# Softmax times values on one core: values of four heads loaded together as 8 KB runs and spread on chip, with exp reading scores in runs of eight

## The chip, the core and the metric

One core of a Trainium2 chip runs the kernel. The metric is the device time of one execution in microseconds (us), as the median of several runs; lower is better. A profile of one further execution, taken by the hardware profiler, gives the times inside a run.

## The reference

There are 8 x 12 = 96 heads. Each has a 1024 x 1024 fp32 matrix of scores (4 MiB) and 1024 x 64 fp32 values (256 KiB). For each head:

```
scores_max = max(scores, axis=-1)
attn = exp(scores - scores_max)
attn = attn / (sum(attn, axis=-1) + 1e-8)
out = attn @ v            # 1024 x 64, fp32
```

All scores are read once, 403 MB; values and outputs are 25 MB each.

## The kernel before

Each head is a stage, and a loop (`tc.For_i`, L209) runs 24 passes of four heads (`AHEAD = 4`). A head's scores lie in one of four buffers `s_nat` as 128 partitions with eight rows each, so one load moves 32 KB in a row to each partition. The head's values lie in one of four buffers `v_sb`: partition p holds value rows 8p to 8p+7, 2 KB in a row (`v_bh`, L41). The outputs go back with 2 KB per partition too.

The work on a head, row group by row group (a group r is one row from each partition):

- ScalarE (ACT, L182) takes exp of two groups at once, from fp32 `s_nat` to fp16 `p_nat`. The maximum is not subtracted; normalization at the end makes up for it. In the last head of a pass the last two groups are exponentiated one by one.
- TensorE (PE, L190) transposes the group in eight 128x128 pieces. Piece c takes every eighth column of the scores, starting at c, so that partition q of the transposed piece stands for key 8q + c, which is the value row that `v_sb` has on partition q at place c.
- VectorE (DVE, L196) copies the eight transposed pieces from PSUM to `pt`.
- PE (L105) multiplies the eight pieces with `vones`, which holds the values in fp16 and a column of ones; the product's last column is the softmax sum.
- For each four groups DVE takes the reciprocal of the sums (L116) and multiplies (L117) into `out_sb`; SyncE (SP, L124) stores a finished head.

GpSimd (POOL, L175) casts each head's values from `v_sb` to `vones`, once per head.

All DMAs are issued by SP, in one queue, in an order that is written out with `queue` (L83). Within a pass it is: values and scores of the next pass's first head, once the first head of this pass has been read; the first output; the same for the second head; outputs two to four; then, at the pass's end (`load_last`, L157), values and scores of the third and the fourth head of the next pass. The last loads of the run are cut: the third head in two pieces, the fourth in four pieces of two row groups, so that work can begin on a part. DMAs use eight completion semaphores in turn, so the issue of a DMA also waits for the landing of the DMA eight places earlier that had the same semaphore.

Of the kernel before, what the change touches and what calls it, by code (L numbers as in the profile page):

```python
# [8 lines left out]
FP32 = mybir.dt.float32  # L9
FP16 = mybir.dt.float16  # L10
# [3 lines left out]
@with_exitstack  # L14
def kernel(
    ctx: ExitStack,
    tc: tile.TileContext,
    scores: bass.AP,
    v: bass.AP,
    out: bass.AP,  # L20
):
    nc = tc.nc
    P = 128

    B, H, SQ, SK = scores.shape
    Bv, Hv, SKv, D = v.shape
    assert (B, H, SK) == (Bv, Hv, SKv)
    BH = B * H
    assert SQ % P == 0 and SK % P == 0
    R = SQ // P  # L30
    C = SK // P
    M = D + 1
    EB = 2
    G = 4
    LAG = 2
    AHEAD = 4

    sc_bh = scores.rearrange("b h (p r) j -> (b h) p r j", p=P)  # L40
    v_bh = v.rearrange("b h (p c) d -> (b h) p c d", p=P)  # L41
    out_bh = out.rearrange("b h (p r) d -> (b h) p r d", p=P)

    const_pool = ctx.enter_context(tc.tile_pool(name="const", bufs=1))
    sb_pool = ctx.enter_context(tc.tile_pool(name="sbpool", bufs=1))
    ps_pool = ctx.enter_context(tc.tile_pool(name="pspool", bufs=1, space=bass.MemoryType.PSUM))

    ident32 = const_pool.tile([P, P], FP32, name="ident32")
    make_identity(nc, ident32)
    ident16 = const_pool.tile([P, P], FP16, name="ident16")  # L50
    nc.vector.tensor_copy(out=ident16[:], in_=ident32[:])  # L51


    vones_bufs = []
    for k in range(AHEAD):
        vo = const_pool.tile([P, C, M], FP16, name=f"vones{k}")
        nc.vector.memset(vo[:, :, D : D + 1], 1.0)  # L57
        vones_bufs.append(vo)

    def buffers(pool, count, shape, dtype, name):
        return [pool.tile(shape, dtype, name=f"{name}{k}") for k in range(count)]

    s_bufs = buffers(sb_pool, AHEAD, [P, R, SK], FP32, "s_nat")
    v_bufs = buffers(sb_pool, AHEAD, [P, C, D], FP32, "v_sb")
    p_bufs = buffers(sb_pool, 8, [P, EB, SK], FP16, "p_nat")
    pt_bufs = buffers(sb_pool, 4, [P, SK], FP16, "pt")
    out_bufs = buffers(sb_pool, 4, [P, R, D], FP32, "out_sb")
    rc_bufs = buffers(sb_pool, 4, [P, G, 1], FP32, "recip")  # L70
    psT_bufs = buffers(ps_pool, 4, [P, SK], FP16, "psT")
    psO_bufs = buffers(ps_pool, 4, [P, G, M], FP32, "psO")
    turn = {}

    def take(bufs):
        k = turn.get(id(bufs), 0)
        turn[id(bufs)] = k + 1
        return bufs[k % len(bufs)]

    pending = []  # L80
    queued = []

    def queue(dma):  # L83

        if queued:
            tc.add_manual_dep(
                dma.ins,
                queued[-1].ins.name,
                mybir.DependencyInfo(mybir.DependencyClass.NoSync, mybir.DependencyReason.DATA),
                reason="queue order",  # L90
            )
        queued.append(dma)

    def one(bh, n):
        return bh[bass.ds(n, 1)].rearrange("o p r d -> (o p) r d")

    def finish(u):

        n, r, pt, st = u
        g = r % G  # L100
        if g == 0:
            st["psO"] = take(psO_bufs)
        psO = st["psO"]
        for c in range(C):
            nc.tensor.matmul(  # L105
                out=psO[:, g, :],
                lhsT=pt[:, c * P : (c + 1) * P],
                rhs=st["vones"][:, c, :],
                start=(c == 0),
                stop=(c == C - 1),  # L110
            )
        if g == G - 1:
            if r == G - 1:
                st["out_sb"] = take(out_bufs)
            recip = take(rc_bufs)
            nc.vector.reciprocal(out=recip[:], in_=psO[:, :, D : D + 1])  # L116
            nc.vector.tensor_tensor(  # L117
                out=st["out_sb"][:, r - G + 1 : r + 1, :],
                in0=psO[:, :, 0:D],
                in1=recip[:].to_broadcast([P, G, D]),  # L120
                op=mybir.AluOpType.mult,
            )
        if r == R - 1:
            dma = nc.sync.dma_start(out=one(out_bh, n), in_=st["out_sb"][:])  # L124
            for other in stores:
                apart(dma, other)
                apart(other, dma)
            apart(dma, dma)
            stores.append(dma)
            queue(dma)  # L130

    stores = []

    def apart(dma, other):
        tc.declare_no_dep(
            dma.ins, other.ins, across_iterations=True, reason="stores of two heads are disjoint"
        )

    def load(k, n, parts=(R,), **cond):
        queue(nc.sync.dma_start(out=v_bufs[k][:], in_=one(v_bh, n), **cond))  # L140
        r = 0
        for rows in parts:
            queue(
                nc.sync.dma_start(  # L144
                    out=s_bufs[k][:, r : r + rows, :],
                    in_=one(sc_bh, n)[:, r : r + rows, :],
                    **cond,
                )
            )
            r += rows  # L150

    def load_next(k, n0):

        if k < AHEAD - 2:
            load(k, (n0 + (AHEAD + k)) % BH, cond=n0 < BH - AHEAD)

    def load_last(n0):  # L157

        before = queued[-1:]

        def loads(parts2, parts3):
            queued[:] = before
            load(AHEAD - 2, (n0 + (2 * AHEAD - 2)) % BH, parts2)
            load(AHEAD - 1, (n0 + (2 * AHEAD - 1)) % BH, parts3)

        with tc.If(n0 < BH - 2 * AHEAD) as cmp:  # L166
            loads((R,), (R,))
        with cmp.Else():
            with tc.If(n0 < BH - AHEAD):
                loads((4, 4), (2, 2, 2, 2))  # L170

    def heads(n0):

        for k in range(AHEAD):
            nc.gpsimd.tensor_copy(out=vones_bufs[k][:, :, 0:D], in_=v_bufs[k][:])  # L175
            st = dict(vones=vones_bufs[k])
            for r in range(R):
                if r % EB == 0:
                    p_nat = take(p_bufs)
                    rows = 1 if k == AHEAD - 1 and r == R - EB else EB  # L180
                    for g in range(0, EB, rows):
                        nc.scalar.activation(  # L182
                            out=p_nat[:, g : g + rows, :],
                            in_=s_bufs[k][:, r + g : r + g + rows, :],
                            func=EXP,
                        )
                p_row = p_nat[:, r % EB, :].rearrange("p (q c) -> p c q", c=C)
                psT = take(psT_bufs)
                for c in range(C):
                    nc.tensor.transpose(  # L190
                        out=psT[:, c * P : (c + 1) * P],
                        in_=p_row[:, c, :],
                        identity=ident16[:],
                    )
                pt = take(pt_bufs)
                nc.vector.tensor_copy(out=pt[:], in_=psT[:])  # L196
                if r == R - 1:
                    load_next(k, n0)
                pending.append((n0 + k, r, pt, st))
                if len(pending) > LAG:  # L200
                    finish(pending.pop(0))
        while pending:
            finish(pending.pop(0))
        load_last(n0)

    assert BH % AHEAD == 0 and BH >= 2 * AHEAD
    for k in range(AHEAD):
        load(k, k)
    with tc.For_i(0, BH, AHEAD, iteration_sync="reg_based") as n0:  # L209
        queued.clear()  # L210
        heads(n0)
# [30 lines left out]
```

## Time and profile before

| | before |
|---|---|
| median of 3 runs | 1068.94 us (1068.86 to 1069.2) |
| the profiled execution: its own time | 1068.56 us |
| the profiled execution: span | 1066.8 us |
| PE busy | 762.6 us (71%) |
| ACT busy | 736.3 us (69%) |
| DVE busy | 609.8 us (57%) |
| POOL busy | 59.9 us (6%) |
| bytes moved by DMA | 453.05 MB, 425 GB/s |
| granted TensorE clock, mean | 0.845 of full speed |

The span runs from the first to the last instruction; the execution's own time also has what lies around it. An engine's busy time is the time that its instructions ran, without waits. The profile shows the DMA engines, of which a core has 16, as packets: a packet is one run of bytes in a row. A DMA over 128 partitions with 2 KB in each has 128 packets of 2 KB. After its packets, each DMA engine writes one packet of 4 bytes, which reports the end. In the views below, "x" with a number counts instructions, "<-" after an idle time names what ended it, and SPq is SP's issue queue.

### The profile page before, as it was taken

The page shows a single profiled execution, that of the slowest core. Times are in us where ns is not written, and L with a number is a line of the kernel's source. Part 1 is how long each engine was busy: PE and PEld are TensorE (multiplying, and loading weights), DVE is VectorE, ACT ScalarE, POOL GpSimd, SP SyncE. Part 2 cuts the span into 40 slices and gives each one's busy share as a digit, 9 for nine tenths or more (in the row PEclk, how much of TensorE's full clock was granted, in tenths as well). Part 3 has the DMA queues.
Part 4 walks back from the last instruction along what each step waited for, and adds up shares of the span by engine and source line. Part 5 has one row for each costly group of instructions (what it writes and reads, how often), then busy time and mean ns, then how long its engine had stood idle before and what let it go on. Part 6 is the DMA issues. An engine that isn't in the chain of part 4 may idle for free.

```text
span 1066.8 us, 32321 instructions
## 1 busy us (share of the span) xinstructions
PE 762.6 (71%) x12288; PEld 722.4 (68%) x12288; DVE 609.8 (57%) x1157; ACT 736.3 (69%) x432; POOL 59.9 (6%) x102
## 2 busy tenths in 40 slices
PE   3766767677776777668686777767776777767777
PEld 3766766677776767667676767767666677767766
DVE  2655555555564655656565565655555555555556
ACT  4757676676867768577676766677766767667686
POOL 0000000000000000000000000000000000000000
PEclk9888888878888888987888798887898788888889
DMA  9999999999999999999999999999999999999996
GB/s 402 424 425 426 432 431 421 437 434 424 429 430 435 423 440 428 430 429 420 439 430 433 424 432 435 430 423 427 436 433 424 439 422 429 428 439 429 431 423 265
DMA packets 42051, 453.05 MB, mean 425 GB/s; under 512 B 4672, under 2 KB 4672, under 8 KB 29248
## 3 DMA queue, kind: packets, MB, share of 16 engines
q1 hardware_dynamic: 42048, 453.00, 99.8%
q8 instruction: 3, 0.05, 0.0%
HBM read 436.73 MB, written 25.17 MB: 433 GB/s over the span
## 4 chain that ended last, share of the span: by engine, by line
DMA 49%; PE 20%; PEld 9%; ACT 8%; DVE 7%; issue 3%; SPq 3%; DVEq 0%; ACTq 0%
DMA s_nat<-in_scores_dram 49%; PE psT L190 13%; ACT p_nat L182 8%; PE psO L105 7%; PEld L190 6%; DVE pt L196 5%; PEld L105 3%; DVE out_sb L117 2%; SPq L140 1%; SPq L124 1%; SPq L144 1%; DVE recip L116 0%; SPq L166 0%; DVEq L196 0%; ACTq L182 0%
## 5 line engine op out<-in xcount | busy, mean ns | idle before, releaser
L182 ACT ACTIVATE p_nat<-s_nat 128x2048 f16<-128x2048 f32 (+1 forms) x408 | 705.5, 1800 | 253.5 <-DMA s_nat<-in_scores_dram 130.6
L190 PE MATMUL psT<-ident,p_nat 128*128 128x128 f16 x6144 | 583.9, 254 | 257.0 <-ACT p_nat L182 256.1
L196 DVE COPY pt<-psT 128x1024 f16<-128x1024 f16 x768 | 519.2, 690 | 429.2 <-PE L190 138.2
L190 PEld LDWEIGHTS <-p_nat 128*128 128x128 f16 x6144 | 501.3, 154 | 274.9 <-ACT p_nat L182 271.1
L105 PE MATMUL psO<-vones,pt 128*128 128x65 f16 x6144 | 375.8, 205 | 41.8 <-DVE pt L196 37.5
L105 PEld LDWEIGHTS <-pt 128*128 128x128 f16 x6144 | 309.0, 107 | 64.0 <-DVE pt L196 60.3
L175 POOL CAST vones<-v_sb 128x512 f16<-128x512 f32 x96 | 59.2, 617 | 987.7 <-PE L105 443.7
L117 DVE TENSOR_TENSOR out_sb<-psO,recip 128x256 f32<-128x256 f32 x192 | 80.8, 421 | 4.2
L182 ACT ACT_TABLE_LOAD x24 | 30.8, 1283 | 69.6 <-DMA s_nat<-in_scores_dram 64.8
L116 DVE RECIPROCAL recip<-psO 128x4 f32<-128x4 f32 x192 | 33.4, 174 | 18.0 <-PE psO L105 18.0
L57 DVE MEMSET vones<- 128x8 f16 x4 | 0.2, 65 | 0.8 <-PEq L226 0.8
L51 DVE CAST ident<-ident 128x128 f16<-128x128 f32 x1 | 0.2, 228 | 0.3 <-POOL ident masks.py:199 0.3
masks.py:199 POOL TENSOR_SCALAR_AFFINE_SELECT ident<-ident 128x128 f32<-128x128 f32 x1 | 0.3, 293 | 0.1
masks.py:197 POOL MEMSET ident<- 128x128 f32 x1 | 0.2, 204 | 0.3 <-POOLq L226 0.3
L226 POOL MEMSET const-float32-0.0<- 128x1 f32 x1 | 0.1, 98 | 0.2 <-issue 0.2
L226 POOL MEMSET const-bfloat16-1.0<- 128x1 bf16 x1 | 0.1, 101 | 0.0
L226 POOL MEMSET const-uint8-127<- 128x1 uint8 x1 | 0.1, 101 | 0.0
L226 POOL MEMSET const-float32-1.0<- 128x1 f32 x1 | 0.1, 98 | 0.0
## 6 DMA issues: line engine op xcount, KB each, us to landing
s_nat<-in_scores_dram SPq DMA_DIRECT2D x96, 4096.0 KB, 27.1
v_sb<-in_v_dram SPq DMA_DIRECT2D x98, 256.0 KB, 20.6
out_dram<-out_sb SPq DMA_DIRECT2D x96, 256.0 KB, 18.0
s_nat<-in_scores_dram SPq DMA_DIRECT2D x2, 2048.0 KB, 19.9
s_nat<-in_scores_dram SPq DMA_DIRECT2D x4, 1024.0 KB, 18.7
```

Of the source, the lines that this page charges most:

```text
L51: nc.vector.tensor_copy(out=ident16[:], in_=ident32[:])
L105: nc.tensor.matmul(out=psO[:, g, :], lhsT=pt[:, c * P : (c + 1) * P], rhs=st["vones"][:, c, :], start=(c == 0), stop=(c == C - 1),)
L116: nc.vector.reciprocal(out=recip[:], in_=psO[:, :, D : D + 1])
L117: nc.vector.tensor_tensor(out=st["out_sb"][:, r - G + 1 : r + 1, :], in0=psO[:, :, 0:D], in1=recip[:].to_broadcast([P, G, D]), op=mybir.Al ...
L124: dma = nc.sync.dma_start(out=one(out_bh, n), in_=st["out_sb"][:])
L140: queue(nc.sync.dma_start(out=v_bufs[k][:], in_=one(v_bh, n), **cond))
L144: nc.sync.dma_start(out=s_bufs[k][:, r : r + rows, :], in_=one(sc_bh, n)[:, r : r + rows, :], **cond,)
L175: nc.gpsimd.tensor_copy(out=vones_bufs[k][:, :, 0:D], in_=v_bufs[k][:])
L182: nc.scalar.activation(out=p_nat[:, g : g + rows, :], in_=s_bufs[k][:, r + g : r + g + rows, :], func=EXP,)
L190: nc.tensor.transpose(out=psT[:, c * P : (c + 1) * P], in_=p_row[:, c, :], identity=ident16[:],)
L196: nc.vector.tensor_copy(out=pt[:], in_=psT[:])
L226: nc = _bacc.Bacc("TRN2", target_bir_lowering=False, num_devices=1)
```

## The change

Four things are changed. `Q` is 32 and `S` is 4.

1. The values of the four heads of a pass are loaded together into one buffer `v_sb` of 128 partitions with 8 KB each: head k lies on partitions 32k to 32k+31, and partition i of these holds value rows 32i to 32i+31. The load is issued as two DMAs of 64 partitions each (`load_v`). It runs a pass further ahead: the values of the pass after the next are loaded at the end of a pass, between the loads of scores three and four, and none are loaded at the end of the last two passes.
2. POOL casts all four heads' values at once to fp16 (`cast_v`), at the end of a pass for the next one. DVE then spreads each head over 128 partitions (`spread_v`) with four copies of 32 partitions each, from `v_half` to `vones`. Partition 32s + i of `vones` then holds rows 32i + 8s to 32i + 8s + 7. The rows of `vones` are padded from 65 to 66 columns, and PE reads the first 65.
3. exp writes its results in the order that fits this placing of the values: for each s of four, it reads runs of eight scores, 32 apart. It reads the same elements with as many instructions.
4. The last head's scores of the run come in pieces of 2, 2, 2, 1 and 1 row groups, instead of 2, 2, 2 and 2.

In the built instruction stream, all 16 copies of the spread stand on DVE ahead of the first copy from PSUM of a pass. PE's instructions stay in their order.

```diff
-    v_bh = v.rearrange("b h (p c) d -> (b h) p c d", p=P)
+    v_bh = v.rearrange("b h (i t) d -> (b h i) (t d)", i=Q)
...
-        vo = const_pool.tile([P, C, M], FP16, name=f"vones{k}")
-        nc.vector.memset(vo[:, :, D : D + 1], 1.0)
+        vo = const_pool.tile([P, C, D + 2], FP16, name=f"vones{k}")
+        nc.vector.memset(vo[:, :, D : D + 2], 1.0)
...
-    v_bufs = buffers(sb_pool, AHEAD, [P, C, D], FP32, "v_sb")
+    v_sb = sb_pool.tile([P, S, C, D], FP32, name="v_sb")
+    v_half = sb_pool.tile([P, S, C, D], FP16, name="v_half")
...
-                rhs=st["vones"][:, c, :],
+                rhs=st["vones"][:, c, 0:M],
...
     def load(k, n, parts=(R,), **cond):
-        queue(nc.sync.dma_start(out=v_bufs[k][:], in_=one(v_bh, n), **cond))
...
+    def load_v(n):
+        rows = v_bh.rearrange("(m g x) y -> m g x y", g=2, x=P // 2)
+        for g in range(2):
+            queue(
+                nc.sync.dma_start(
+                    out=v_sb[g * (P // 2) : (g + 1) * (P // 2)].rearrange("x s c d -> x (s c d)"),
+                    in_=rows[bass.ds(n // AHEAD, 1), g].rearrange("o x y -> (o x) y"),
+                )
+            )
+
+    def cast_v():
+        nc.gpsimd.tensor_copy(out=v_half[:], in_=v_sb[:])
+
+    def spread_v(k):
+        for s in range(S):
+            nc.vector.tensor_copy(
+                out=vones_bufs[k][s * Q : (s + 1) * Q, :, 0:D],
+                in_=v_half[k * Q : (k + 1) * Q, s],
+            )
...
-        def loads(parts2, parts3):
+        with tc.If(n0 < BH - 2 * AHEAD) as cmp:
             queued[:] = before
-            load(AHEAD - 2, (n0 + (2 * AHEAD - 2)) % BH, parts2)
-            load(AHEAD - 1, (n0 + (2 * AHEAD - 1)) % BH, parts3)
-
-        with tc.If(n0 < BH - 2 * AHEAD) as cmp:
-            loads((R,), (R,))
+            load(AHEAD - 2, (n0 + (2 * AHEAD - 2)) % BH)
+            load_v((n0 + 2 * AHEAD) % BH)
+            load(AHEAD - 1, (n0 + (2 * AHEAD - 1)) % BH)
         with cmp.Else():
             with tc.If(n0 < BH - AHEAD):
-                loads((4, 4), (2, 2, 2, 2))
+                queued[:] = before
+                load(AHEAD - 2, BH - 2, (4, 4))
+                load(AHEAD - 1, BH - 1, (2, 2, 2, 1, 1))
...
-            nc.gpsimd.tensor_copy(out=vones_bufs[k][:, :, 0:D], in_=v_bufs[k][:])
+            spread_v(k)
...
                         nc.scalar.activation(
-                            out=p_nat[:, g : g + rows, :],
-                            in_=s_bufs[k][:, r + g : r + g + rows, :],
+                            out=p_nat[:, g : g + rows, :].rearrange(
+                                "p r (s v) -> p s r v", s=S
+                            ),
+                            in_=s_bufs[k][:, r + g : r + g + rows, :].rearrange(
+                                "p r (i s c) -> p s (r i) c", s=S, c=C
+                            ),
                             func=EXP,
                         )
...
         while pending:
             finish(pending.pop(0))
+        cast_v()
         load_last(n0)
...
+    load_v(0)
     for k in range(AHEAD):
         load(k, k)
+    cast_v()
+    load_v(AHEAD)
     with tc.For_i(0, BH, AHEAD, iteration_sync="reg_based") as n0:
```

## The prediction

> **What bounds the kernel now.** I read the page's DMA part first, since the engine shares (PE 71%, ACT 69%, DVE 57%) name no engine that is full.
>
> ```profile
> DMA packets 42051, 453.05 MB, mean 425 GB/s; under 512 B 4672, under 2 KB 4672, under 8 KB 29248
> ...
> q1 hardware_dynamic: 42048, 453.00, 99.8%
> ...
> DMA 49%; PE 20%; PEld 9%; ACT 8%; DVE 7%; issue 3%; SPq 3%; DVEq 0%; ACTq 0%
> ...
> L182 ACT ACTIVATE p_nat<-s_nat 128x2048 f16<-128x2048 f32 (+1 forms) x408 | 705.5, 1800 | 253.5 <-DMA s_nat<-in_scores_dram 130.6
> ```
>
> The packets of one queue fill the 16 DMA engines for 99.8% of the span: that is the bound. The chain of waits gives DMA only 49% because it names the instruction that ended each wait; a queue that never runs dry hides behind whatever compute ran meanwhile. The largest part of ACT's idle time ends with a scores landing. Next, two loop passes of four heads as windows, and the end of the run:
>
> ```profile
> core 0: us, PE busy (x) PEld busy (x) DVE busy (x) ACT busy (x) POOL busy (x), PEclk, DMA share, GB/s
> 499.40:543.30 43.90, 32.41 (x513) 30.62 (x513) 25.37 (x48) 30.68 (x19) 2.47 (x4) 0.81 1.01 430
> 543.30:587.20 43.90, 32.47 (x513) 30.90 (x513) 25.56 (x48) 30.67 (x19) 2.47 (x4) 0.81 1.01 430
> 1020.00:1066.80 46.80, 32.97 (x573) 30.88 (x571) 28.84 (x56) 31.74 (x19) 1.85 (x3) 0.90 0.80 335
> ```
>
> A pass takes 43.9 us with the DMA share at 1.01 and no engine over 33 us. 24 passes x 43.9 = 1053.6 us of the 1066.8 us span.
>
> The trace's packet records turn this into a price list. From one packet's start to the next on the same DMA engine (median): 80 ns for 2 KB, 306 ns for 8 KB, 607 ns for 16 KB, 1210 ns for 32 KB, 6 ns for the 4-byte packet that ends a DMA on an engine. (Their durations, 84, 309, 611 and 1213 ns, overlap by some 4 ns; I count intervals.) So a packet costs about 4.8 ns plus its bytes at 27.2 GB/s. The sum for one engine: 1536 x 80 + 32 x 306 + 16 x 607 + 752 x 1210 + 292 x 6 = 1054.0 us, which agrees with 24 passes.
>
> Last, how much lateness the queue forgives. SP's own timeline at a pass's end, then the chain:
>
> ```profile
> 531.22 11.05 SPq L124 DMA_DIRECT2D out_dram<-out_sb  x3
> 542.75 0.35 SPq L140 DMA_DIRECT2D v_sb<-in_v_dram  x1
> 543.41 0.35 SPq L144 DMA_DIRECT2D s_nat<-in_scores_dram  x1
> ```
> ```profile
> 543.41 19.80 DMA s_nat<-in_scores_dram
> ```
>
> The load issued at 543.41 lands 19.80 us later, but its packets take 8 x 1.21 = 9.7 us: it queued about 10 us. The engines' landings for one DMA spread over 2.35 us there, so the earliest engine has about 7.7 us of work left when the pass's last compute releases this load. Compute may be that much later at no cost.
>
> [...] Before has only 128-partition DMAs[...]; it does show each engine at 27.2 GB/s in all of them[...].
>
> **The change, part by part.**
>
> *Bytes in larger packets.* Per pass the four value loads go from 4 x (8 x 80 + 6) = 2584 ns per engine to 8 x 306 + 2 x 6 = 2460 ns, if a packet to 64 partitions runs as one to 128. That is -0.12 us x 24 = -2.98 us. The 8 KB price comes from before's own quarter loads of the last head.
>
> *Two halves of 64 partitions.* This is the disputed cost. Lower bound: nothing (-2.98 us stands; a gain below nothing is excluded, as the bytes are the same). Upper bound: [...] each 8 KB packet takes 612 ns: 8 x 306 = 2.45 us more per pass, 24 x 2.45 = 58.8 us. Could unlike engine phases save it? [...] The landing records show 12 of 16 engines within 0.35 us of each other, against the 1.22 us that half a load takes at full rate. So most are in step, and the slowest sets the pace since a DMA is complete only when all have landed. I take the upper bound[...]: -2.98 + 58.8 = +55.8 us. Nothing covers it: the queue is the bound.
>
> *Issue and waits.* A pass issues 10 DMAs instead of 12, and SP reuses 8 completion semaphores in turn. In the built order the next pass's first scores load waits for the second value half, queued before scores load 3: 9.7 us of queue remains, against 10.3 before (the value and scores load then left). The first output store waits for load 3, and the second scores load is issued behind it with one scores load (9.7 us) still to run. The second value half waits for the next first scores load: by the chain's rhythm it lands at 583.9, and that issue comes at about 588. 4 us to spare. No cost; if this cover went, each us of lateness is a us per pass.
>
> *The cast.* One POOL cast of 128x2048 replaces four of 617 ns: 4 x 617 = 2.5 us, while POOL idles 94% of the time. It depends on values loaded a pass earlier and the spreads of the current pass, so it ends long before its readers. No cost. SP's value load queues behind it and finds it done.
>
> *The spread.* 16 DVE copies of 32x512 per pass, all ahead of the pass's first pt copy on DVE. Not in before's trace. [...] I take 4 us. Behind them wait the pt copies, then PE. DVE has 43.9 - 25.4 = 18.5 us idle per pass, and a head arrives each 10.3 to 11 us and needs 8.1 us of PE (32.4/4): two to three us are recovered per head, so 4 us is gone before the fourth head, whose end releases the loads. [...] No cost.
>
> *The exp in runs of eight.* Same elements, read 32 bytes at a time. [...] the trace has 1901[...]. Lower bound 0[...]; upper: half rate, 3.6 us. I take 0. ACT has 30.7 of 43.9 us, so it decides only from about 2.6 us on.
>
> *The tail.* The last landing is followed by 9.5 us of compute and store. Before, the last quarter's two rows are exponentiated together after it:
>
> ```profile
> 1057.39 2.01 ACT L182 ACTIVATE p_nat<-s_nat 128x1024 f16<-128x1024 f32 x2 [0.63 <-PE L105]
> ```
>
> With the quarter split, row 6 lands 1.2 us earlier and ACT is free at 1056.8, so row 7's exp starts at about 1057.85 instead of 1058.4: -0.5 us. The additional DMA costs 0.04 us. The larger first value load delays the first head by 1.8 us, with the queue full: no cost.
>
> **Sum.** The profiled execution took 1068.56 us, 1.76 above its span and 0.38 below the median of the runs, 1068.94. 1068.56 + 55.8 - 0.5 = 1123.9; on the median, 1124.
>
> **Rivals.**
> 1. *The halves cost nothing.* [...] Then 1068.94 - 2.98 - 0.5 = 1065.5, faster by 0.3%. For it: the packet price list, with no unknown in it. [...] It decides if a value packet takes under 322 ns: 0.12 us per pass spread on 8 packets is 16 ns each.
> 2. *Half the conflict.* Engines drift apart [...]: 1068.94 - 3.5 + 29.4 = 1095. For it: four engines stand 1.8 to 2.3 us behind the twelve. Against: the twelve.
> 3. *ACT becomes the bound.* At half rate a pass is 15 x 3.6 + 2 x 1.9 + 1.3 = 59.1 us, 24 x 59.1 + 15 = 1433. Against: [...] before already has 13 us of slack.
>
> **How the numbers follow.** Full conflict 0.53 (own range 1110 to 1130), rival 1 0.33, rival 2 0.10, rival 3 or a stall at the pass's start 0.04. About 0.2% is what a measurement of this kernel can tell from no change: rival 1 straddles it, 0.26 beyond, 0.07 within. So faster 0.26, same 0.07, slower 0.67. The range runs from rival 1 to the full conflict, 1064.5 to 1130; both ends are needed, since leaving out either case leaves out over 2 in 10.
>
> **What would show it.** Right: value packets near 612 ns, passes of 46.2 us, DMA share still at 1, scores packets near 1210 ns except next to a value load. Wrong in the main step: value packets at 306 to 309 ns and passes of 43.8 us. The spread is right if DVE adds 3 to 6 us per pass and no queue gap follows; the exp if ACT stays at 1.9 us. A DMA share well below 1 in mid-run would mean that a wait which I costed at nothing starves the queue.

## The result and the profile after

The changed kernel takes 1249.85 us, the median of 4 runs (1246.33 to 1261.86); the kernel before took 1068.90 us in 4 runs beside it. The ratio is 1.1712, with a 95% interval of 1.163 to 1.1795. The forecast of 1124.0 had the direction right and was far too small; the time lies outside its range. The profiled execution took 1246.33 us with a span of 1244.5, 177.7 us more than the span before.

The page of the changed kernel, in the parts that answer to those of before (the DMA counts, the queue, the chain by engine, and the groups of exp, spread and cast):

```profile
DMA packets 32212, 453.05 MB, mean 364 GB/s; under 512 B 3921, under 2 KB 3921, under 8 KB 16465
...
q1 hardware_dynamic: 32208, 453.00, 96.6%
...
DMA 67%; PE 11%; PEld 5%; SPq 4%; ACT 4%; DVE 4%; issue 3%; DVEq 0%; ACTq 0%
...
L209 ACT ACTIVATE p_nat<-s_nat 128x2048 f16<-128x2048 f32 (+1 forms) x408 | 705.2, 1800 | 418.1 <-DMA s_nat<-in_scores_dram 359.7
...
L174 DVE COPY vones<-v_half 32x512 f16<-32x512 f16 x384 | 109.5, 285 | 36.3 <-DVE out_sb L123 12.4
...
L169 POOL CAST v_half<-v_sb 128x2048 f16<-128x2048 f32 x25 | 47.4, 1894 | 1180.0 <-DVE recip L122 547.8
```

The same bytes move at 364 GB/s instead of 425, yet the queue's packets still fill 96.6% of the span. So most of the added time lies in packets that take longer, and a smaller part in engines that have no packet to move, which I call dry (by the packet records 42.5 us per engine, 3.4% of the span; before, 1.8 us). Exp is no slower, 1800 ns in the mean as before, and ACT's added idle time ends with scores landings (359.7 us, before 130.6). The share of DMA in the chain rises from 49% to 67%: compute now really waits.

Two passes in the middle and the end of the run, as windows with the columns shown in the prediction:

```profile
core 0: us, PE busy (x) PEld busy (x) DVE busy (x) ACT busy (x) POOL busy (x), PEclk, DMA share, GB/s
506.60:557.70 51.10, 33.15 (x512) 31.55 (x512) 29.97 (x64) 30.68 (x19) 1.90 (x1) 0.77 0.98 370
557.70:608.70 51.00, 33.30 (x512) 31.69 (x512) 29.98 (x64) 30.66 (x18) 1.89 (x1) 0.77 0.99 369
1190.00:1244.50 54.50, 38.50 (x649) 35.90 (x649) 36.52 (x78) 38.06 (x23) 1.89 (x1) 0.84 0.72 290
```

A pass takes 51.0 us instead of the 43.9 of before and the 46.2 that the forecast implies. PE and ACT have the busy time of before; DVE has 4.5 us more, the spread. SP's own timeline at a pass's end, then the chain there:

```profile
508.11 11.19 SPq L130 DMA_DIRECT2D out_dram<-out_sb  x3
519.87 0.36 SPq L149 DMA_DIRECT2D s_nat<-in_scores_dram  x1
520.60 1.49 SPq L162 DMA_DIRECT2D v_sb<-in_v_dram  x2
522.47 26.16 SPq L149 DMA_DIRECT2D s_nat<-in_scores_dram  x2
557.70 0.37 SPq L130 DMA_DIRECT2D out_dram<-out_sb  x1
```
```profile
522.47 35.11 DMA s_nat<-in_scores_dram
```

The pass's fourth scores load is issued at 522.47. The second load of that line is the next pass's first, and SP can't issue it until about 548.6: it shares its semaphore with the second half of the values, which has not landed. SP's waits of this kind over the whole run (total, times, longest, in us):

```profile
SPq L149 <- DMA v_sb<-in_v_dram: 381.7, 21, 20.0
```

The load of 522.47 lands 35.1 us after its issue, where the corresponding one of before took 19.8 us.

The packet records say where the time lies. A DMA has one 4-byte packet on each engine (before: 4672 of them, and as many landings, for 292 DMAs). For each size I sum the durations, subtract the count times the undisturbed duration (9 ns for 4 bytes, 84.5 for 2 KB, 159 for 4 KB, 309 for 8 KB, 611 for 16 KB, 1214 for 32 KB) and divide by the 16 engines. "Not busy" is the span minus the sum of all packets per engine. "Spread" is the time between the first and the last engine's landing of one DMA, as the median of all DMAs. In us:

| kernel | 8 KB packets | 32 KB packets | other packets | not busy | spread |
|---|---|---|---|---|---|
| before | 0 | 0 | 0 | 1.8 | 2.4 |
| after | +51.9 | +90.2 | +0.8 | 42.5 | 8.2 |
| e1, full width | 0 | 0 | +0.3 | 7.6 | 2.8 |
| e2, one DMA | +0.7 | +38.6 | -0.3 | 51.6 | 0.5 |
| e3, every second partition | +0.5 | +0.4 | -0.4 | 8.8 | 2.7 |
| e4, before with halves | +0.4 | +42.0 | +12.0 | 12.3 | 1.4 |
| e5, halves early | +49.4 | +42.6 | +4.5 | 40.1 | 10.2 |
| e9, half the bytes | 0 | +52.6 | +37.5 | 22.3 | 8.8 |
| e12, halves last | +47.2 | +39.6 | +0.2 | 18.3 | 0.6 |

("Other" is mostly the values where these come as 2 or 4 KB packets: +11.2 in e4, +36.9 in e9.) For the change the books close: 51.9 + 90.2 + 0.8 + (42.5 - 1.8) and -5.9 for the larger packets (undisturbed durations 1059.1 against 1065.0 us per engine) make 177.7 us, the difference of the spans.

So the value packets cost about what was forecast: their median is 602 ns, where 612 was forecast (588 ns over all 8 KB packets, as some of the last head's scores also come in this size). What was not forecast is in the other two columns: scores packets, 90.2 us, and engines that run dry, 40.7 us.

### The profile page after: what moved, and what is told of

Read it like the earlier page. It is cut to its first block, busy times and chain, and to the rows that moved or that the text cites. A ratio compares the mean times of both kernels' runs of the same rounds, so it can differ in the third digit from the quotient of the medians.

```text
span 1244.5 us, 32741 instructions
## 1 busy us (share of the span) xinstructions
PE 795.8 (64%) x12288; PEld 754.6 (61%) x12288; DVE 719.2 (58%) x1541; ACT 736.0 (59%) x432; POOL 48.1 (4%) x31
## 3 DMA queue, kind: packets, MB, share of 16 engines
q1 hardware_dynamic: 32208, 453.00, 96.6%
## 4 chain that ended last, share of the span: by engine, by line
DMA 67%; PE 11%; PEld 5%; SPq 4%; ACT 4%; DVE 4%; issue 3%; DVEq 0%; ACTq 0%
DMA s_nat<-in_scores_dram 67%; PE psT L221 7%; ACT p_nat L209 4%; PE psO L111 4%; PEld L221 3%; SPq L162 2%; DVE pt L227 2%; PEld L111 2%; DVE out_sb L123 2%; SPq L149 1%; SPq L130 1%; DVE vones L174 0%; DVE recip L122 0%; SPq L188 0%; DVEq L227 0%
## 5 line engine op out<-in xcount | busy, mean ns | idle before, releaser
L209 ACT ACTIVATE p_nat<-s_nat 128x2048 f16<-128x2048 f32 (+1 forms) x408 | 705.2, 1800 | 418.1 <-DMA s_nat<-in_scores_dram 359.7
L221 PE MATMUL psT<-ident,p_nat 128*128 128x128 f16 x6144 | 611.3, 262 | 339.6 <-ACT p_nat L209 329.2
L221 PEld LDWEIGHTS <-p_nat 128*128 128x128 f16 x6144 | 523.8, 155 | 354.0 <-ACT p_nat L209 351.7
L111 PE MATMUL psO<-vones,pt 128*128 128x65 f16 x6144 | 385.8, 209 | 103.9 <-DVE pt L227 101.7
L111 PEld LDWEIGHTS <-pt 128*128 128x128 f16 x6144 | 318.6, 110 | 130.5 <-DVE pt L227 128.7
L174 DVE COPY vones<-v_half 32x512 f16<-32x512 f16 x384 | 109.5, 285 | 36.3 <-DVE out_sb L123 12.4
L169 POOL CAST v_half<-v_sb 128x2048 f16<-128x2048 f32 x25 | 47.4, 1894 | 1180.0 <-DVE recip L122 547.8
## 6 DMA issues: line engine op xcount, KB each, us to landing
s_nat<-in_scores_dram SPq DMA_DIRECT2D x2, 2048.0 KB, 18.3
s_nat<-in_scores_dram SPq DMA_DIRECT2D x2, 512.0 KB, 19.8
```

The costliest lines, as they stand in the source:

```text
L111: nc.tensor.matmul(out=psO[:, g, :], lhsT=pt[:, c * P : (c + 1) * P], rhs=st["vones"][:, c, 0:M], start=(c == 0), stop=(c == C - 1),)
L169: nc.gpsimd.tensor_copy(out=v_half[:], in_=v_sb[:])
L174: nc.vector.tensor_copy(out=vones_bufs[k][s * Q : (s + 1) * Q, :, 0:D], in_=v_half[k * Q : (k + 1) * Q, s],)
L209: nc.scalar.activation(out=p_nat[:, g : g + rows, :].rearrange("p r (s v) -> p s r v", s=S), in_=s_bufs[k][:, r + g : r + g + rows, :].rea ...
L221: nc.tensor.transpose(out=psT[:, c * P : (c + 1) * P], in_=p_row[:, c, :], identity=ident16[:],)
```

## The experiments

Three theories were on the table. A: what hurts is that a load goes to a contiguous block of 64 partitions; its packets crowd each other and the scores packets beside them. B: the cost comes from the rest of the change (cast, spread, order of exp, number of DMAs and their semaphores). C: it comes from loads of 64 rows with 8 KB packets, whichever partitions they go to. Later ones are named where they came up. The kernel before took 1068.99 to 1069.05 us (medians) beside these runs.

### e1: the same bytes, place and semaphores, but each DMA over 128 partitions

```diff
-        rows = v_bh.rearrange("(m g x) y -> m g x y", g=2, x=P // 2)
+        rows = v_bh.rearrange("(m x) (s y) -> m x s y", x=P, s=S)
...
-                    out=v_sb[g * (P // 2) : (g + 1) * (P // 2)].rearrange("x s c d -> x (s c d)"),
-                    in_=rows[bass.ds(n // AHEAD, 1), g].rearrange("o x y -> (o x) y"),
+                    out=v_sb[:, 2 * g : 2 * g + 2].rearrange("x s c d -> x s (c d)"),
+                    in_=rows[bass.ds(n // AHEAD, 1), :, 2 * g : 2 * g + 2].rearrange("o x s y -> (o x) s y"),
```

> The change with one edit: the group's values still come in two DMAs at the same place of the queue and with the same semaphores, but each covers all 128 partitions with half the bytes (4 KB), not 64 partitions with 8 KB. Theory A [...]: everything above before goes away, passes of 43.8 us, 4 KB packets at 159 ns, 32 KB packets back at 1213 ns, about 1066 us. Rival B (the fewer semaphores per pass, the cast, the spread on DVE or the exp order starve the queue): all of that is still there, so it stays near 1250 us.

Measured: 1070.21 us (12 runs), ratio 1.0012 [1.0003, 1.0021]. The queue and two passes of e1:

```profile
q1 hardware_dynamic: 35280, 453.00, 99.3%
```
```profile
core 0: us, PE busy (x) PEld busy (x) DVE busy (x) ACT busy (x) POOL busy (x), PEclk, DMA share, GB/s
497.80:541.60 43.80, 31.96 (x512) 30.22 (x510) 29.69 (x65) 30.62 (x18) 1.90 (x1) 0.81 1.01 431
541.60:585.40 43.80, 32.06 (x531) 30.08 (x530) 30.61 (x66) 30.69 (x19) 1.89 (x1) 0.84 1.01 431
```

Cast, spread, order of exp, tail and the number of DMAs are all as in the change, and a pass takes 43.8 us. B falls: none of these parts costs a mid-run pass anything, and 180 us hang on the partitions of one DMA. (Theory A said about 1066 us, 4 us less than came; the same holds for e3, and where these microseconds stayed is the subject of the last section of experiments.)

### e3: 64 rows of 8 KB, but on every second partition

```diff
-        rows = v_bh.rearrange("(m g x) y -> m g x y", g=2, x=P // 2)
+        rows = v_bh.rearrange("(m x g) y -> m g x y", g=2, x=P // 2)
...
-                    out=v_sb[g * (P // 2) : (g + 1) * (P // 2)].rearrange("x s c d -> x (s c d)"),
+                    out=v_sb[g : P : 2].rearrange("x s c d -> x (s c d)"),
```

> The change with each half transfer on every second partition instead of on a block of 64: still 64 partitions, 8 KB packets, two DMAs, the same semaphores, but partitions of all 128 are reached by each. Theory A: [...] about 1066 us; [...] 8 KB packets still at about 600 ns and a time between 1120 and 1250. Rival C (a transfer on 64 partitions is slow whatever partitions these are): near 1250 us.

Measured: 1069.52 us (12 runs), ratio 1.0006 [0.9997, 1.0014]; 8 KB packets take 309 ns in the median, scores packets 1213. The queue of e3:

```profile
q1 hardware_dynamic: 32208, 453.00, 99.2%
```

SP's wait for the second value half is still there, and costs no pass anything (a pass takes 43.8 us):

```profile
SPq L149 <- DMA v_sb<-in_v_dram: 253.5, 22, 11.6
```

The packets are as many and as large as in the change, in as many DMAs with the same semaphores; their partitions differ, and with them the rows that one DMA reads from memory, every second 8 KB instead of 512 KB in a row. That reading in a row is not what costs: e2, below, reads 1 MiB in a row at 309 ns a packet. C falls and A holds: of the two outcomes that it allowed here, about 1066 us and 1120 to 1250 us, the time is near the first. The 8 KB packets take 311 ns in the mean, against 549 in the change. Why a block of 64 neighbouring partitions slows them is not shown: no record here names what these packets share.

### e4: the kernel before, with each head's values in two halves

```diff
-        queue(nc.sync.dma_start(out=v_bufs[k][:], in_=one(v_bh, n), **cond))
+        for g in range(2):
+            half = slice(g * (P // 2), (g + 1) * (P // 2))
+            queue(nc.sync.dma_start(out=v_bufs[k][half], in_=one(v_bh, n)[half], **cond))
```

> The kernel before with one edit: each head's value load is issued as two DMAs of 64 partitions each, in 2 KB packets, 16 DMAs per pass. Nothing else of the change is in it. Theory A: the same bytes as in the change go through half-width transfers, so 2 KB packets rise from 84 to about 160 ns and the scores beside them suffer: at least 24 x 2.6 = 62 us more, 1130 us or above. Rival B: 1069 to 1071 us (only 4 x 6 ns more completions per pass).

Measured: 1140.72 us, ratio 1.068 [1.0657, 1.0703]. Two passes of e4:

```profile
core 0: us, PE busy (x) PEld busy (x) DVE busy (x) ACT busy (x) POOL busy (x), PEclk, DMA share, GB/s
500.00:546.60 46.60, 32.77 (x512) 31.48 (x512) 25.47 (x48) 30.68 (x18) 2.48 (x4) 0.82 1.03 413
546.60:593.20 46.60, 32.00 (x512) 30.25 (x512) 25.38 (x48) 30.67 (x18) 2.48 (x4) 0.82 1.01 408
```

Halves alone, with the same bytes of values, cost 71.7 us (65.7 in the profiled execution), and the DMA share of these passes stays at 1.01 or above: in mid-run it is crowding. 11.2 + 42.0 us of longer packets are near the 58.8 us that the forecast priced for halves. The 10.5 us by which its engines are dry for longer are a stall in the last pass, where PE waits 12.2 us for a POOL cast (the kind that e7, below, shows). In e4, where the load of one half is short (128 KB), most of the crowding falls on the scores packets (+42.0 us), and less on the 2 KB packets (+11.2): their mean is 92 ns, values and outputs together, where the theory had 160 for the values. The change pays 109 us more than this for the same values.

### e9: half the bytes in halves

```diff
-        rows = v_bh.rearrange("(m g x) y -> m g x y", g=2, x=P // 2)
+        rows = v_bh.rearrange("(m g x) (s y) -> m g x s y", g=2, x=P // 2, s=S)
...
-                    out=v_sb[g * (P // 2) : (g + 1) * (P // 2)].rearrange("x s c d -> x (s c d)"),
-                    in_=rows[bass.ds(n // AHEAD, 1), g].rearrange("o x y -> (o x) y"),
+                    out=v_sb[g * (P // 2) : (g + 1) * (P // 2), 0:2].rearrange("x s c d -> x (s c d)"),
+                    in_=rows[bass.ds(n // AHEAD, 1), g, :, 0:2].rearrange("o x s y -> (o x) (s y)"),
...
+        rows = v_bh.rearrange("(m x) (s y) -> m x s y", x=P, s=S)
+        queue(
+            nc.sync.dma_start(
+                out=v_sb[:, 2:4].rearrange("x s c d -> x (s c d)"),
+                in_=rows[bass.ds(n // AHEAD, 1), :, 2:4].rearrange("o x s y -> (o x) (s y)"),
+            )
+        )
```

> The change with half as many bytes in its half transfers: each of the two 64-partition DMAs carries 4 KB per partition, and a third DMA brings the other 4 KB to all 128 partitions. Eleven DMAs per pass; the next scores load still waits for the second half transfer. Theory A (the cost is that of crowded bytes, once in the late engine's own values and once in its scores beside the others' values): about half of the 178 us, 1145 to 1175 us. Rival (a fixed cost per half transfer, or the waits alone): 1230 us or above.

Measured: 1177.6 us, ratio 1.102 [1.1004, 1.1037]. Half of the bytes in halves bring 108.6 of 181 us, 60%, just above the 1145 to 1175 us of theory A and far from the rival's 1230. The cost grows with the bytes sent in halves; it isn't a price per DMA. But it is more than half, and the spread (8.8 us) is that of the change, so a part may come with the first crowded load. (A third value DMA also moves the semaphores by one place, so the comparison is not pure.)

### e2: one DMA over 128 partitions

```diff
-        rows = v_bh.rearrange("(m g x) y -> m g x y", g=2, x=P // 2)
-        for g in range(2):
-            queue(
...
+        rows = v_bh.rearrange("(m x) y -> m x y", x=P)
+        queue(
+            nc.sync.dma_start(
+                out=v_sb[:].rearrange("x s c d -> x (s c d)"),
+                in_=rows[bass.ds(n // AHEAD, 1)].rearrange("o x y -> (o x) y"),
+            )
+        )
```

> The change with the two half transfers replaced by a single one over 128 partitions with 8 KB each: nine DMAs per pass instead of ten, so that the next pass's first scores load takes the semaphore that the fourth scores load had before it, and must wait until that has landed. Theory A: packets at 309 and 1213 ns, as in e1; but the queue is empty when that wait ends, so each of 23 passes loses the time from a landing to the next first packet, some 2 us and what the engines are apart, 2 to 5 us: 1115 to 1180 us. If the number of DMAs per pass doesn't matter, about 1065 us. Rival B: near 1250 us.

Measured: 1151.14 us, ratio 1.0764 [1.0746, 1.0782], although its value packets take 309 ns. SP's timeline at a pass's end of e2, then SP's waits (total, times, longest, in us):

```profile
536.97 0.35 SPq L161 DMA_DIRECT2D v_sb<-in_v_dram  x1
537.66 33.57 SPq L149 DMA_DIRECT2D s_nat<-in_scores_dram  x2
571.46 0.36 SPq L130 DMA_DIRECT2D out_dram<-out_sb  x1
```
```profile
SPq L149 <- DMA s_nat<-in_scores_dram: 485.3, 25, 21.5
```

With nine DMAs in a pass instead of ten, the next pass's first scores load shares its semaphore with the fourth scores load, which is the last in the queue. SP therefore issues it only when the queue is empty, once per pass, and the queue starts again from nothing: 51.6 us not busy, 2.15 us a pass (51.6 / 24). The 32 KB packets cost 38.6 us more without any crowding. Two packets of each engine and pass make nearly all of it: the first after the pause (mean 1884 ns in the pass at 570 us) and the last of the second scores load (2072 ns, on all 16 engines at once), (0.67 + 0.86) x 24 = 36.7 us. The second of these I can't explain; kernels whose queue doesn't run dry (e1, e3) don't have it. The time lies within the 1115 to 1180 us of theory A, but that had the scores packets at 1213 ns and all the loss in the pauses. So a DMA that is left out can cost 82 us, and the semaphores decide it. It also warns of the +90.2 us of the change: a part of it may be such restarts and not crowding (e12 comes back to this).

### e5: the halves early in the pass, behind the second scores load

Theory A1, a narrower A: what the change pays beyond the packets themselves comes from where the halves stand, ahead of the fourth load, so that the next scores load waits for them.

```diff
-    def load_v(n):
+    def load_v(n, **cond):
...
+        if k == 1:
+            load_v((n0 + 2 * AHEAD) % BH, cond=n0 < BH - 2 * AHEAD)
...
-            load_v((n0 + 2 * AHEAD) % BH)
...
         for k in range(AHEAD):
             spread_v(k)
+        cast_v()
+        for k in range(AHEAD):
...
-        cast_v()
         load_last(n0)
```

(The edit in words: the call moves from the end of a pass to the second head, and the cast stands right behind the spreads.)

> The change with its half transfers kept as they are, but issued behind the second scores load of a pass, so that no scores load takes the semaphore of a half transfer (the first one of the next pass now takes that of the third scores load). The cast follows the spreads directly. Theory A1 (two costs: the crowding itself, about 55 to 60 us as in e4, and the queue running dry while the next scores load waits for the engine that lands its half last, the rest): 1125 to 1150 us, DMA share of the engines back near 99%. Theory A2 (the crowding alone costs all of it, because engines that are apart crowd each other more): stays near 1250 us.

Measured: 1199.15 us, ratio 1.1215 [1.1174, 1.1256]. A pass of e5:

```profile
core 0: us, PE busy (x) PEld busy (x) DVE busy (x) ACT busy (x) POOL busy (x), PEclk, DMA share, GB/s
513.00:562.60 49.60, 32.96 (x512) 31.54 (x512) 29.84 (x65) 30.93 (x20) 1.89 (x1) 0.79 0.99 386
```

50.7 us of the cost go with the place, but the rest stays well above 1125 to 1150 us, the engines are still dry for 40.1 us (the queue's share is 96.6%, as in the change), and their landings are 10.2 us apart. A1 isn't enough.

### What the records of one engine show

I followed the engine that lands last through the changed kernel, packet by packet, each one's end matched to the next one's start. From 580.46 to 632.11 us, one pass, it has no pause. Its packets there make 43.7 us undisturbed, and 8.0 us more: 3.6 us in the third scores load, while other engines write values,

```
third scores load, ns:  1213 1213 1506 2369 2214 2388 1215 1213
```

1.9 us in its own value packets, and 2.4 us in the other scores loads. The sum is the pass, 51.65 us. The other engines have finished by then and stand dry, as the next load isn't issued before this engine has landed its values. The landings show that it is one engine: the second value half of this pass lands from 588.3 us on, on fifteen engines within 3.6 us, and on the last one 10.9 us after the first. So theory S: one engine far behind sets the pace; it meets the others' crowded phase with scores packets, pays there as well as in its own, and the rest wait. The spread supports it: it grows from 0.4 us at the start of the run over 2.4 and 5.9 to 7 to 13 us, and stays there. Within a pass it grows by some 4 us while values are written (7.0 to 10.9 us in this one) and shrinks by some 3 us until the next ones. Pass lengths grow with it, from 48.1 us early to about 53 us at the end.

### e12: the halves last, so that all engines start each pass in step

```diff
             load(AHEAD - 2, (n0 + (2 * AHEAD - 2)) % BH)
-            load_v((n0 + 2 * AHEAD) % BH)
             load(AHEAD - 1, (n0 + (2 * AHEAD - 1)) % BH)
+            load_v((n0 + 2 * AHEAD) % BH)
```

The next pass's first scores load then waits for the first half, behind which only the second is queued. S says that the lag can't build up, and the other theories that the longer wait makes it worse.

> The change with the two half transfers moved behind the fourth scores load of a pass. The next scores load now waits for the first half, with only the second half left in the queue, so that the engines run dry and start again together in every pass, as in e2. Theory S (what makes the change cost 178 and not 60 us is that one engine falls far behind and then meets the others' values with its scores, and their scores with its values): the engines stay within some 1 us, 32 KB packets are slow only where they start after a pause, 8 KB packets cost some 50 us as before; with e2's 82 us for running dry that makes 1190 to 1215 us, less than the change, although its queue runs dry in every pass. Rival (engines in step crowd each other no less): crowding as in the change, 143 us of longer packets, and running dry on top, above 1270 us.

Measured: 1171.23 us, ratio 1.0961 [1.0943, 1.0979]: 79 us less than the change, below what S expected (1190 to 1215), and far from the rival's over 1270. The queue, two passes, and SP's waits of e12:

```profile
q1 hardware_dynamic: 32208, 453.00, 98.4%
```
```profile
core 0: us, PE busy (x) PEld busy (x) DVE busy (x) ACT busy (x) POOL busy (x), PEclk, DMA share, GB/s
500.00:596.00 96.00, 66.12 (x1031) 62.93 (x1030) 59.61 (x128) 61.81 (x37) 3.79 (x2) 0.78 0.99 393
```
```profile
SPq L149 <- DMA v_sb<-in_v_dram: 454.7, 21, 22.7
```

SP waits longer in all than in the change (454.7 us against 381.7), and yet the engines are less often dry (18.3 us against 42.5): they end within 0.6 us of each other, and the second half is still queued when the wait for the first one ends. The value packets take 604 ns in the median, close to twice 306, and cost +47.2 us in all. The +39.6 us of the scores packets are mostly restarts as in e2: the first packet after the pause takes 1870 ns, the last of the second scores load 2180 ns, and (0.66 + 0.97) x 24 = 39 us.

The packet records also divide the +90.2 us of the change. I sort the scores packets by whether a value packet is in flight on any engine for more than 0.3 us of their time, and sum what they take beyond 1214 ns:

| kernel | scores packets beside values | the other scores packets |
|---|---|---|
| after | +50 us | +40 us |
| e2, one DMA | 0 | +39 us |
| e12, halves last | +5 us | +35 us |

So the change's 40 us beside no values are as much as the restarts of e2 cost, and the other 50 us are crowding that nearly vanishes once the engines are in step. In e12, with the engines in step, crowding costs near what the forecast said and falls almost wholly on the value packets (+47.2 us, and +5 us on scores beside them); the queue's restart in each pass costs 35 us (e12) and 39 us (e2) in packets, and 16.5 us (e12) to 49.8 us (e2) in dry engines; and what the change pays beyond these comes with the engine that falls behind. S expected at least 19 us more than came, as it charged e2's 82 us in full, with 33 us more of dry engines than e12 has; it had the direction and not the size.

### e7: the tail alone, in the kernel before

```diff
-                loads((4, 4), (2, 2, 2, 2))
+                loads((4, 4), (2, 2, 2, 1, 1))
```

> The kernel before with only the last head's scores in pieces of 2, 2, 2, 1 and 1. The prediction's step: 0.5 us less than before, 1068.4 us. Rival: in the last pass PE sets the pace and not the last landing, so nothing: 1068.9 us.

Measured: 1080.85 us, ratio 1.0109 [1.0094, 1.0125], 11.8 us slower. SP's waits and those of PE and POOL in e7's last pass, then SP's timeline:

```profile
SPq L140 <- DMA s_nat<-in_scores_dram: 18.3, 1, 18.3
...
PE psO L105 <- POOL vones L175: 12.3, 1, 12.3
...
POOL vones L175 <- DMA s_nat<-in_scores_dram: 31.9, 1, 31.9
```
```profile
1057.97 0.10 SPq L140 DMA_DIRECT2D v_sb<-in_v_dram  x1
1058.62 0.08 SPq L144 DMA_DIRECT2D s_nat<-in_scores_dram  x1
1058.95 0.36 SPq L124 DMA_DIRECT2D out_dram<-out_sb  x1
1060.76 14.87 SPq L124 DMA_DIRECT2D out_dram<-out_sb  x3
```

The last pass's loads are skipped by their condition, but the instruction is still there with its wait. One DMA more moved the semaphores by one place, so that the skipped value load (0.10 us at 1057.97) waited 18.3 us for the last piece of scores. Behind it in SP's order stands the first output (1058.95, before at 1046.96), and a POOL cast waited too, and PE for it. The gain of 0.5 us could not show in any case: in before, e1 and e3 the last exps wait for PE, not for a landing. In the change the same pieces meet other semaphores; what they cost there wasn't measured alone, but its last pass shows no stall of this size (39.7 us from ACT's last table load to DVE's end; before, 38.8).

### Where e3's saving of 3.4 us went: e6, e8, e10, e11

e3 is the change without the crowding, and the forecast for that case was 1065.5 us. The starts of ACT's table loads mark the passes. Against before, e3 is 2.74 us later at the start of its third pass, wins 3.37 us over the next 21 passes (43.765 us each against 43.925), and its last pass, to the start of DVE's last instruction, takes 40.79 us against 38.33. 2.74 - 3.37 + 2.46 = 1.83, and the profiled runs differ by 1.82 (1070.38 and 1068.56). The last pass of before, then that of e3:

```profile
core 0: us, PE busy (x) PEld busy (x) DVE busy (x) ACT busy (x) POOL busy (x), PEclk, DMA share, GB/s
1023.50:1061.90 38.40, 30.08 (x514) 28.30 (x512) 25.56 (x50) 30.96 (x18) 1.85 (x3) 0.91 0.86 361
1022.90:1063.70 40.80, 31.24 (x544) 29.06 (x541) 31.46 (x68) 30.68 (x18) 1.90 (x1) 0.87 0.77 326
```

DVE does 5.9 us more in e3's last pass, 4.56 of them the 16 copies at its start, and with a DMA share of 0.77 the queue isn't the bound there. Theory D: these copies cost the end. e8 orders the copies of heads two to four behind the sixth `pt` copy of the head before.

```diff
-            nc.vector.tensor_copy(
+            copy = nc.vector.tensor_copy(
...
+            if k > 0:
+                tc.add_manual_dep(
+                    copy.ins,
+                    pt_copies[-3].ins.name,
+                    mybir.DependencyInfo(mybir.DependencyClass.NoSync, mybir.DependencyReason.DATA),
+                    reason="spread order",
+                )
```

e6 is the kernel of e3 once more. Its one run took 1068.96 us. It says nothing on D, but how far such sums can be trusted: its passes are as e3's (43.764 us), while its start is 2.50 us late and its last pass takes 39.60 us, 1.27 us more than before and not 2.46.

> The kernel of e3 once more, one look beside the others of this call, so that they are compared on the same chip: 1069 to 1070 us.

> The kernel of e3, with the spreads of heads two to four put behind the sixth copy from PSUM of the head before, instead of all ahead of the pass's first one. Theory D (in the last pass compute sets the end, and the 4.5 us of spreads at its start are lost there): about 2 us less than e3, 1067 to 1068 us. Rival (the spreads are hidden in every pass): as e3, 1069.5 us.

Measured for e8: 1069.88 us (13 runs), ratio 1.0008 [1.0, 1.0016]. D is right on the last pass (38.08 us) and gains nothing where it had 1067 to 1068 us: the passes take 43.91 us again, and one engine's lag grows from 1.9 to 4.8 us through the run. Why late copies lengthen the passes stays open.

e10 is e3 with the values of the next pass loaded right behind its first scores load, not a pass further ahead, so that the start carries 1 MiB less; e11 adds e8's order.

```diff
+        if k == 0:
+            load_v((n0 + AHEAD) % BH, cond=n0 < BH - AHEAD)
...
-            load_v((n0 + 2 * AHEAD) % BH)
...
+        cast_v()
         for k in range(AHEAD):
             spread_v(k)
...
-        cast_v()
         load_last(n0)
...
-    cast_v()
-    load_v(AHEAD)
```

> The kernel of e3 with the values loaded no further ahead than before: for the next pass, right behind its first scores load, and cast and spread at that pass's start. Theory E (in e3, 1 MiB of values loaded a pass earlier takes 2.5 us ahead of all later scores, which is where the saving of the larger packets went): about 2 us less than e3, 1067 us. Rival (the last pass is set by compute anyway, and the cast of 1.9 us now lies in its path): 1069 to 1071 us.

> The kernel of e10 with the spreads of heads two to four put later, as in e8. If the spreads at the start of the last pass cost anything there: up to 2 us less than e10, 1065 to 1067 us. Rival: no change from e10.

Measured: e10 1070.32 us (13 runs), ratio 1.0012 [1.0003, 1.002]; e11 1070.05 us (13 runs), ratio 1.0012 [1.0004, 1.002]. Theory E falls. e10 is 1.70 us later than before at its third pass instead of 2.74, keeps the 3.37 us of the passes, and loses 3.4 us in the last pass (41.74); its time lies in the rival's 1069 to 1071 us. e11 has the short last pass (38.32) and the long passes (about 43.93). No version beats the kernel before: some 3.4 us are won in the passes of e3, e6 and e10, and each arrangement gave them back at one of the run's ends or in the passes. These are single executions, and differences of about 1 us between them are within what e3 and e6, the same kernel, show.

## Why the prediction was wrong, step by step

**The sum.** It foresaw +55.3 us of span; 177.7 came, 122.4 us more. By the table: value packets -6.9 (51.9 against 58.8), scores packets +90.2, dry engines +40.7, larger packets and small ones -2.1 (-5.1 by durations, which overlap, against -2.98 by intervals), the tail's +0.5 that was subtracted. Two terms that the sum set at zero, scores packets and dry engines, make the whole miss.

**What bounds the kernel.** Right: the DMA queue; e1 and e3 show that the added on-chip work changes no mid-run pass.

**Bytes in larger packets.** Right: -0.12 us a pass forecast, -0.16 in e3.

**Two halves of 64 partitions.** The price was right in size (602 ns in the change and 604 in e12, 612 forecast), and so was the choice of the upper bound over rival 1. That choice was an estimate, twice the 306 ns of before; before has no load to 64 partitions, so its trace gave no reason to choose it. That the slowest engine sets the pace, before does show: the load issued at 543.41 lands on the engines from 560.86 to 563.21, and its exp starts at 563.32. What failed in this step is "So most are in step": it was read from before, where nothing pushes the engines apart. In the changed kernel they drift apart while values are written, to a spread of 8.2 us in the median. So scores packets run beside value packets, which the sum didn't charge: some 50 us. Rival 2 thought that engines out of step would pay less; out of step they paid more (+50 us on scores packets beside values, +5 in e12), as scores packets of some meet the value packets of others.

**Issue and waits.** This step failed most. It saw the wait, "the next pass's first scores load waits for the second value half", and covered it with the 9.7 us of queue that remain behind that half: "No cost". An engine that lands early uses up this queue while the last one is still at its values; the forecast itself had taken the 2.35 us of before off its 10 us to get 7.7. The half that lands from 588.3 us on has a spread of 10.9 us, more than all of the 9.7, and the load that waits for it (381.7 us of waits in 21 passes) finds the early engines dry. That is the 40.7 us of dry engines, and restarts behind such pauses would be of the size of the remaining 40 us of scores packets (39 in e2). (The step's 4 us to spare belong to another wait, that of the second value half itself for a scores load; SP's waits at the value loads come to 6.2 us in the whole run.) In e3 the same wait, for the same DMA, lasts 253.5 us in all and costs no pass anything: the wait was there in both, the cover only in one. The step's own reservation, "each us of lateness is a us per pass", is what came. What the prediction said would show this, a DMA share well below 1 in mid-run, came only as 0.98: a mean over 16 engines hides that one of them never pauses.

**The cast, the exp.** Right: 1894 ns on an idle POOL (2.5 us estimated), and exp at 1901 ns for 2048 elements as before; that the runs of eight would add nothing was an estimate, without a measurement. Rival 3 is out.

**The spread.** 16 x 285 = 4.56 us a pass (4 taken, an estimate without a measurement), hidden in mid-run as said. The last pass was not costed: there the whole pass is 1.3 us (e6) to 2.5 us (e3) longer; e8, with most copies later, has the last pass of before.

**The tail and the start.** -0.5 us did not come; in before the same edit costs 11.8 us through a semaphore (e7). "The larger first value load" was said to cost nothing, but e3 is 2.7 us late at its third pass, where 1 MiB of values loaded a pass earlier stands ahead of the scores (some 2.5 us by the forecast's own price). What part of it is these bytes is not shown: e10, which doesn't load them early, is still 1.7 us late.

**What stays open.** Which engine falls behind first and why; why the spread stays at 1.4 us in e4, whose halves are short, and reaches 8 to 10 in the change, e5 and e9; whether the 40 us of the change's scores packets beside no values are all restarts, as their size in e2 and e12 suggests; why a restart also lengthens the last packet of the second scores load; and why a load to 64 neighbouring partitions is slow at all, which no record shows.

## What to carry to other kernels

Look at which partitions one DMA covers before its packet size: here two loads a pass to 64 neighbouring partitions cost 180 us in all, where two loads over every second partition cost nothing. The 9.7 us of queue that were to cover a wait did so in e3, whose engines land 2.7 us apart in the median, and not in the change, where they came 10.9 us apart, so a change that sets DMA engines against each other must be charged for the slack it uses up, with the slowest engine and not the mean. And count DMAs per pass against the completion semaphores before one is added or taken away: it cost 82 us in e2 and 11.8 us in e7, with the same bytes moved.

## What the runs showed of the hardware that was not expected

- A 64-row load on every second partition ran at the rate of a 128-row load: 8 KB packets at 309 ns in e3, as in e2, against 602 on a block of 64 (value packets of the change).
- A 32 KB packet that starts after a pause of the queue takes about 1880 ns without any crowding, against 1213, and another one some 20 us later 2070 to 2180 ns (e2, e12); the first 2 KB packets of a run take about 610 ns, against 84 (before).
- A DMA that its condition skipped still waited for its semaphore, 18.3 us in e7.
- In the change, the engine that has fallen behind stays behind: the landing spread grows from 0.4 us to 7 to 13 us within seven passes, although the others run dry in every pass; it shrinks by some 3 us (10.9 to 8.0 in the pass from 580 us), and the next values bring that back (12.0).
